# A hybrid attention and delta-rule layer: queries loaded two tiles ahead, the attention's other loads spread over its tiles, three differences of the last stage back in their place

## The chip, the cores and the metric

One core of one Trainium2 chip. The metric is the device time of one execution in microseconds (us); the kernel before takes 1301.49 us, the median of 3 runs (1301.42 to 1302.32).

## What is computed

One layer over a sequence of 1024 positions of width 1024. A normalised input goes through one projection; its columns feed two mixers, a banded attention (8 heads of 64, each chunk of 64 positions sees itself and 8 chunks before, with a learned bias by distance) and a gated delta rule (4 heads of 128, a recurrence over chunks). Their outputs are joined and projected, and a feed-forward with a squared ReLU follows:

```python
u = rms_norm(h, mix_norm_gain[layer])
proj = u @ w_in[layer]
...
mixed = jnp.concatenate([o_att, o_dn], axis=-1) @ w_out[layer]
h = h + mixed
z = rms_norm(h, ffn_norm_gain[layer]) @ w_ff1[layer]
h = h + jnp.square(jax.nn.relu(z)) @ w_ff2[layer]
```

In the attention, per head: scores of normalised q and k, plus the bias, masked to the band, softmax, times v.

## The kernel before, in words

The kernel runs in stages on the one core: the projections (to about 361 us), attention and delta rule together (to about 575), the output projection (to about 671), the first matrix of the feed-forward (ff1, to about 977) and the second (ff2, to about 1290), then the last outputs. Large products are made of three matmuls each: an operand is split into a high part (a cast on ScalarE, line 204, the names that end in _h) and a low part (the difference on VectorE, line 205, names in _l), and high x high, high x low and low x high are summed.

**What orders the work.** TensorE's (PE's) instructions run in the order in which the kernel writes them. VectorE (DVE), ScalarE (ACT), GpSimd (POOL) and SyncE (SP, which issues nearly all DMAs) are ordered by a scheduler behind the kernel, which works from where an instruction is written, from its inputs and from the tile buffers that it needs. Each engine then works through its own list in order: an instruction that waits holds up all that stand behind it on that engine. With `tc.issue_after(x)` the kernel makes an instruction wait in that order for x.

**Attention (`attention`).** The heads are worked in two groups g = 0, 1, the positions in eight tiles t of 128; a tile (g, t) is named t00 to t17. For a tile, `start` (line 885) loads the queries t.._q: two DMAs of 256 KB from q_dr, into a buffer of which there are two (only t11 has another place). For each half pp of a tile, `score` makes the scores on PE (line 916, t.._sb and t.._sa, with the keys ks), VectorE and ScalarE make the softmax, PE transposes it (lines 976 and 992, t.._tpb, t.._tpa), multiplies by the values vt (line 1015, t.._o), and turns the output (line 1037, t.._on). Between these stand the steps of the delta rule: merges of triangular blocks (m.., l.., among them m1_tp at lines 674 and 676 and l_p at line 641), and the chunk steps (c0 to c7, among them c_pv at line 517, which reads c_jv).

The order of all of this on PE comes from a planner, written out in a loop over a modelled clock: at each turn it lists what could be done (score, flip, multiply, delta steps and others), with a modelled time at which each can begin, and takes the one that can begin first, or the one of highest rank of those that can. For a score that time is when its PSUM banks are free; for the very first one it is at least START, 5000 ns. `start` is called when the first half of the tile is scored, so a tile's query load is written right ahead of its first scores. At tile t02 the planner also calls `load_rest`, which writes all at once: the older biases of group 0 (biaso00 to 03), values vt2 and vt3, keys ks010 to ks013, values vt4 to vt7, keys ks100 to ks103 and ks110 to ks113. Each of the ks and vt loads is 256 KB. At t06 follow the biases of group 1.

**ff2 (`ff2`).** The 4096 inner positions are worked in four blocks kb = 0 to 3. In each the 2 x 2 block product is made of seven products instead of eight, from sums and differences of the blocks: p1, p5, p2, p3, p6, p7, p4, in this order, each of 48 matmuls (line 1430) over two halves i = 0, 1. Operands are called after product, block, side and half: p50b0_l is the low part of side b of product p5, block 0, half 0. `prep5` makes s1 = a21 + a22 and b11 = b12 - b11, `prep3` makes s1 = s1 - a11 (line 1514) and a12 = a12 - s1, `prep7` makes a21 = a11 - a21 (line 1524) and b12 = b22 - b12, all on VectorE in place, each 128 x 1024. `early` is the last split of p5: the differences of lines 1514 and 1524 are held back until that split has been issued. While block 0 begins, the last steps of ff1 still run on VectorE and ScalarE (yy7, and its store f_dr<-yy), and the loads of block 0 come in.

Of the kernel before, what the change touches and what calls it, by code (L numbers as in the profile page):

```python
# [40 lines left out]
DELTA = 71e3  # L41
LATENCY, MARGIN = 250, 400
LEAD = 0.1
START = 5000
NV = 6


# [52 lines left out]
def hymba_kernel(  # L100
# [729 lines left out]
    def attention(after, delta, values, outputs):  # L830
# [16 lines left out]
        def load_old(g):  # L847
            for i in range(4):
                b = bias_page("u", f"biaso{g}{i}")
                nc.sync.dma_start(out=b[:, 0:384], in_=bias_win[4 * g + i, :, 0:384])  # L850
                nc.gpsimd.memset(b[64:128, 0:64], NEG)
                old[g].append(b)
# [13 lines left out]
                nc.sync.dma_start(out=tl, in_=v_dr[t])  # L866
                vt.append(tl)

        def load_rest():
            load_old(0)  # L870
            load_values((2, 3))
            load_keys(0, 1)
            load_values(range(4, NT))
            load_keys(1, 0)
            load_keys(1, 1)

        keys, old, new, vt = [[[], []], [[], []]], [[], []], [[], []], []
        load_keys(0, 0)
        load_new(0)
        load_values((0, 1))  # L880

        tiles, outs = {}, {}

        def start(g, t):
            n = f"t{g}{t}"
            T = dict(n=n, k0=max(0, t - 4))
            T["kb"] = max(0, t - 1)
            if (g, t) == (1, 1):
                T["q"] = [page("on", f"{n}_q{m}", F32R) for m in range(2)]
                for r0 in (0, 64):  # L890
                    for m in range(2):
                        nc.sync.dma_start(out=T["q"][m].bitcast(F32)[r0:r0 + 64], in_=q_dr[t, :, m, g, :])
            else:
                q = page("x", n + "_q", F32R, w=DM)
                qf = q.bitcast(F32)
                for r0 in (0, 64):
                    nc.sync.dma_start(out=qf[r0:r0 + 64].rearrange("p (m c) -> p m c", m=2), in_=q_dr[t, :, :, g, :])
                T["q"] = [part(q, m) for m in range(2)]
            T["sums"] = small("t", n + "_sum", 8)
            T["nm"] = small("t", n + "_nm", 8)  # L900
            T["s"], T["p"], T["done"] = {}, {}, {}
            tiles[g, t] = T

        def product(g, T, i, bk, off, ka, kb):
# [157 lines left out]
        total, spent, deltas, begun, multiplied = sum(size), 0, 0, 0, 0  # L1062
        ready, later, live = [], [], {}
        banks = clock.banks
        groups = delta
        fed = next(groups)

# [15 lines left out]
        while True:  # L1083
            if not any(k in live for k in "MSOF") and fed is not None:
                fed = next(groups, None)
                for k, gen in (fed or {}).items():
                    live_add(k, gen)
                continue
            todo = []
            lag = deltas < DELTA * (spent / total + LEAD)  # L1090
            for r, k in enumerate("SMOF"):
                if k in live:
                    todo.append((at(live[k][1]), (0 if lag else 6) + 0.1 * r, k))
            if multiplied < len(ready):
                t = max(ready[multiplied:multiplied + 2])
                if multiplied + 2 <= len(ready):
                    todo.append((max(t, banks["o"][0]), 1, "multiply"))
            for p in later[:1]:
                todo.append((max(p[0], banks["t"][0]), 2, "later"))
            if flipping is None and flipped < begun and flipped - multiplied < 2:  # L1100
                flipping = flip(*units[flipped])
                flipping = flipping, next(flipping)
            if flipping is not None:
                todo.append((at(flipping[1]), 3, "flip"))
            if begun < len(units) and begun - multiplied < 5 and (begun - flipped < 3):
                a = banks["a"]
                todo.append((max(a[0], a[1] - 500, a[2] - 900, START if not begun else 0), 4, "score"))
            if values_left:
                todo.append((banks["a"][0], 7, "values"))
            elif flipped == len(units) and not live.keys() - {"F"} and not any(p[1] is finish and p[2][1] < NT - 1 for p in later):  # L1110
                if outputs_gen is None:
                    outputs_gen = outputs()
                if fill < 30 and (multiplied < len(units) or later or live):
                    todo.append((banks["a"][0], 8, "outputs"))
            if not todo or (len(todo) == 1 and todo[0][2] == "outputs"):
                break
            best = min(todo, key=lambda p: (max(p[0] - clock.now, 0), p[1]))
            if best[0] > clock.now:
                clock.now = best[0]
            k = best[2]  # L1120
            if k in live:
                gen = live[k][0]
                before = clock.now
                want = next(gen, None)
                deltas += clock.now - before
                if want is None:
                    del live[k]
                else:
                    live[k] = gen, want
            elif k == "multiply":  # L1130
                for n in units[multiplied:multiplied + 2]:
                    multiply(*n)
                    pe(218 * size[multiplied])
                pe(300)
                spent += 2 * size[multiplied]
                t = give("o", on("s", 366, clock.now + LATENCY, ahead=True))
                later.append((t, finish, units[multiplied][0:2]))
                multiplied += 2
            elif k == "later":
                _, step, args = later.pop(0)  # L1140
                step(*args)
                if step is finish:
                    t = give("t", on("v", 420, pe(220), ahead=True))
                    if args[0]:
                        t = on("v", 853, on("g", 3200, on("s", 780, t)))
                        later.append((t + MARGIN, turn, args[1:]))
                        later.sort(key=lambda p: p[0])
                else:
                    give("t", on("v", 682, pe(440), ahead=True))
            elif k == "flip":  # L1150
                want = next(flipping[0], None)
                flipping = want and (flipping[0], want)
                if want is None:
                    flipped += 1
            elif k == "score":
                g, t, pp = units[begun]
                if pp == 0:
                    start(g, t)
                    if (g, t) == (0, 2):
                        load_rest()  # L1160
                    if (g, t) == (0, 6):
                        load_new(1)
                        load_old(1)
                score(g, t, pp)
                begun += 1
            elif k == "values":
                if next(values, None) is None:
                    values_left = False
                else:
                    give("a", on("s", 690, pe(5500)))  # L1170
            else:
                next(outputs_gen)
                pe(690)
                fill += 1
# [231 lines left out]
    def ff2(psw, pools):  # L1406
# [7 lines left out]

        y = {i: [wide(t, 0), wide(t, 1)] for i, t in y.items()}
        y[7] = [page2("y7", f"y7_{i}") for i in range(2)]
        side, splits = [0], []
# [4 lines left out]
        def product(name, prep, by_rows=False):  # L1422
# [11 lines left out]
            for i in range(2):  # L1434
                ab = []
                for o, src in zip("ab", prep(i)):
                    hi = page2("h" + t, f"{name}{o}{i}_h", F32R)
                    lo = page2("l" + t, f"{name}{o}{i}_l", F32R)
                    splits.append(split(src, hi, lo, nc.scalar, nc.vector)[1])
                    ab.append((hi, lo))  # L1440
                ops.append(ab)
                if not by_rows:
                    for k in range(2):
                        for q in range(4):
                            step(i, k, q)
# [13 lines left out]
        for kb in range(nb):  # L1459
# [50 lines left out]
                return s1[i], b11[i]  # L1510

            def prep3(i):
                with tc.issue_after(early):
                    tt(s1[i], s1[i], a11[i], ALU.subtract)
                tt(a12[i], a12[i], s1[i], ALU.subtract)
                return a12[i], b22[i]

# [2 lines left out]
                return s1[i], b11[i]  # L1520

            def prep7(i):
                with tc.issue_after(early):
                    tt(a21[i], a11[i], a21[i], ALU.subtract)
                tt(b12[i], b22[i], b12[i], ALU.subtract)
                return a21[i], b12[i]

# [3 lines left out]

            accumulate(1, product(f"p1{kb}", lambda i: (a11[i], b11[i])))
            accumulate(5, product(f"p5{kb}", prep5))
            early = splits[-1]
            accumulate(2, product(f"p2{kb}", lambda i: (a12[i], b21[i])))
            if last:
                merge(nc.gpsimd, 2, 1)
# [124 lines left out]
```

## Time and profile before

| | |
|---|---|
| median of 3 runs | 1301.49 us |
| the profiled execution | 1301.99 us |
| its span, first to last instruction | 1300.1 us |
| granted TensorE clock, mean | 0.984 |
| PE busy | 1252.7 us (96%) |
| VectorE busy | 931.8 us (72%) |
| ScalarE busy | 546.5 us (42%) |
| GpSimd busy | 289.9 us (22%) |
| mean DMA rate | 122 GB/s |

All times are us from the start of the span. A row of the waits names the engine and line that waited, what it waited for, the total, the number of times and the longest. A row of the timeline gives start, duration, engine, line, operation, output<-input by the program's names, and the count where like instructions are put together; the brackets hold the idle time of the engine ahead of it and what ended it. In the trace's rows buffer numbers are left out, so t_q is any tile's query page and ks any key page; matmuls overlap, so that a matmul of 0.39 us may start 0.23 us behind the one ahead. A row of the windows gives the stretch, its length, the busy time of each engine with the number of instructions, PE's granted clock (1.00 is full, 0.50 half), the busy share of the DMA engines and their rate.

### The profile page before, as it was taken

How to read it: one execution, taken by the hardware profiler on the slowest of the kernel's cores; microseconds unless marked ns; L12 is line 12 of the kernel's file. 1: busy time of each engine (PE TensorE's matmuls, PEld its weight loads, DVE VectorE, ACT ScalarE, POOL GpSimd, SP SyncE). 2: the span in 40 equal slices, each digit the busy share in tenths (PEclk: the TensorE clock that was granted, in tenths of full speed). 3: DMA queues.
4: the chain of work that ended last, by engine and by line, in shares of the span. 5: the costliest groups of instructions: out<-in, count | busy, mean ns of one | idle time of the engine just before them, and what ended most of it. 6: DMA issues, size and time to landing. Idle time of an engine off the chain costs nothing.

```text
span 1300.1 us, 18013 instructions
## 1 busy us (share of the span) xinstructions
PE 1252.7 (96%) x6686; PEld 1043.8 (80%) x6686; DVE 931.8 (72%) x1389; ACT 546.5 (42%) x898; POOL 289.9 (22%) x487
## 2 busy tenths in 40 slices
PE   9999999999979999879999999999999899999998
PEld 7778878788868988757878788888888688888886
DVE  7899978655036577662529876776668888897998
ACT  7233232232246556463436445444445343333331
POOL 4425451454013344543220000000000000000034
PEclk9999999999979999899999999999999899999999
DMA  6214354566564542123351433332259423413002
GB/s 221 68 47 143 95 150 128 100 169 171 166 210 103 160 105 76 32 85 130 109 169 46 151 118 125 101 114 93 97 194 352 166 97 126 134 61 125 9 33 97
DMA packets 135399, 158.53 MB, mean 122 GB/s; under 512 B 31760, under 2 KB 79376, under 8 KB 134800
## 3 DMA queue, kind: packets, MB, share of 16 engines
q1 hardware_dynamic: 117216, 135.11, 33.9%
q10 hardware_dynamic: 18096, 22.29, 5.0%
q8 instruction: 52, 0.85, 0.3%
q14 instruction: 35, 0.29, 0.1%
HBM read 109.91 MB, written 47.45 MB: 121 GB/s over the span
## 4 chain that ended last, share of the span: by engine, by line
PE 47%; DVE 8%; DMA 3%; ACT 2%; issue 2%; POOL 1%; POOLq 1%; SPq 0%; DVEq 0%; ACTq 0%
PE q L1334 19%; PE p L1430 19%; PE op L223 6%; DMA b<-f_dr 1%; DMA y<-h_dr 1%; PE t_o L1015 1%; DVE h L1276 1%; POOLq L1657 1%; DVE y L1502 0%; DMA h_dr<-h 0%; DVE q_0a_l L205 0%; DMA a<-in_w_ff_dram 0%; PE t_sa L916 0%; DVE y L1498 0%; ACT t_pb L955 0%
## 5 line engine op out<-in xcount | busy, mean ns | idle before, releaser
L1502 POOL TENSOR_TENSOR y<-y,y 128x1024 f32<-128x1024 f32 x6 | 19.3, 3240 | 596.5 <-DVE y L1498 577.7
L1498 DVE TENSOR_TENSOR y<-y,p 128x1024 f32<-128x1024 f32 x46 | 55.3, 1218 | 9.3 <-PE p L1430 8.4
L936 DVE CUSTOM_DVE_ANT_0 t_pb<-t_sb,biasn 128x256 f32<-128x256 f32 (+1 forms) x64 | 23.4, 404 | 41.8 <-PE t_sb L916 41.7
L223 PE MATMUL op<-mh,wo_h 128*128 128x512 f32 x128 | 50.8, 397 | 2.5 <-ACT mh L204 1.1
L223 PE MATMUL op<-ml,wo_h 128*128 128x512 f32 x128 | 50.8, 396 | 0.9 <-DVE ml L205 0.9
L223 PE MATMUL op<-mh,wo_l 128*128 128x512 f32 x128 | 49.3, 394 | 0.5 <-DVE wo_l L205 0.5
L955 ACT ACTIVATE t_pb<-t_pb,t_nm 128x256 f32<-128x256 f32 (+1 forms) x64 | 31.3, 489 | 37.8 <-DVE t_nm L947 34.4
L1221 POOL TENSOR_TENSOR op_q<-op_q 128x512 f32<-128x512 f32 x14 | 20.9, 1496 | 51.4 <-ACT op_q L1220 51.3
L916 PE MATMUL t_sb<-ks,t_q 128*128 128x256 f32 (+1 forms) x144 | 25.6, 310 | 7.0 <-DMA t_q<-q_dr 7.0
L992 PE MATMUL t_tpa<-ident,t_pa 128*128 128x128 f32 x120 | 21.7, 288 | 10.8 <-ACT t_tb L982 6.1
L1214 DVE TENSOR_TENSOR h<-op,op_x 128x512 f32<-128x512 f32 x16 | 11.0, 689 | 28.3 <-PE op L223 28.2
L223 PEld LDWEIGHTS op<-mh,wo_h 128*128 128x128 f32 x128 | 24.2, 189 | 8.7 <-ACT mh L204 1.6
L223 PEld LDWEIGHTS op<-mh,wo_l 128*128 128x128 f32 x128 | 24.3, 190 | 6.6 <-DVE wo_l L205 1.4
L223 PEld LDWEIGHTS op<-ml,wo_h 128*128 128x128 f32 x128 | 24.3, 190 | 6.1 <-DVE ml L205 1.2
L959 ACT ACTIVATE t_pa<-t_pa,t_nm 128x384 f32<-128x384 f32 (+2 forms) x48 | 26.3, 548 | 0.0
L223 PE MATMUL g_ps<-uh,wg_h 128*128 128x512 f32 x64 | 25.3, 396 | 1.0 <-ACT wg_h L204 1.0
L916 PEld LDWEIGHTS t_sb<-ks,t_q 128*128 128x128 f32 x144 | 20.4, 206 | 7.3 <-issue 7.1
L223 PE MATMUL g_ps<-uh,wg_l 128*128 128x512 f32 x64 | 25.2, 393 | 0.4 <-POOL wg_l L205 0.4
L223 PE MATMUL dq_ps<-uh,wdq_h 128*128 128x512 f32 x64 | 25.5, 398 | 0.0
L223 PE MATMUL aq_ps<-waq_h,uh 128*128 128x512 f32 x64 | 25.5, 401 | 0.0
L947 DVE CUSTOM_DVE_ANT_0 t_pa<-t_sa,biaso,t_nm 128x384 f32<-128x384 f32 (+2 forms) x48 | 24.9, 545 | 0.8 <-PE t_o L1015 0.6
L223 PE MATMUL dv_ps<-uh,wdv_l 128*128 128x512 f32 x64 | 25.4, 397 | 0.0
(1109 smaller groups left out, 4333.3 us busy)
## 6 DMA issues: line engine op xcount, KB each, us to landing
wa<-in_w_ff_dram SPq DMA_DIRECT2D x32, 512.0 KB
a<-in_w_ff_dram SPq DMA_DIRECT2D x32, 512.0 KB
b<-f_dr SPq DMA_DIRECT2D x32, 512.0 KB
f_dr<-yy ACTq DMA_DIRECT2D x16, 512.0 KB
t_q<-q_dr SPq DMA_DIRECT2D x30, 256.0 KB
f_dr<-zz ACTq DMA_DIRECT2D x13, 512.0 KB
ks<-k_dr SPq DMA_DIRECT2D x16, 256.0 KB
wo_r<-in_w_out_dram SPq DMA_DIRECT2D x16, 256.0 KB
```

The costliest lines, as they stand in the source:

```text
L223: nc.tensor.matmul(ps, a, b, start=(first and i == 0), stop=(last and i == n - 1))
L916: nc.tensor.matmul(o, q[m][:, i * P:(i + 1) * P], k[:, c], start=(m == 0), stop=(m == 1))
L936: nc.vector.tensor_tensor_reduce(sb[:, c], bk[:, c], new[g][pp][:, c], -1.0, 3.0e38, ALU.add, ALU.min, nm[:, 4 + i:5 + i])
L947: nc.vector.tensor_tensor_reduce(sa[e][:, 0:wa], bk[:, 0:wa], old[g][i][:, 384 - wa:384], -1.0, nm[:, 4 + i:5 + i], ALU.add, ALU.min, nm[: ...
L955: nc.scalar.activation(sb[:, c], sb[:, c], AF.Exp, bias=m, scale=-1.0, accum_out=T["sums"][:, 4 + i:5 + i])
L959: nc.scalar.activation(sa[e][:, 0:wa], sa[e][:, 0:wa], AF.Exp, bias=m, scale=-1.0, accum_out=T["sums"][:, i:i + 1])
L992: nc.tensor.transpose(tp[:, js], sa[e][:, js], ident)
L1221: nc.gpsimd.tensor_tensor(acc, acc, sq, ALU.add)
L1334: nc.tensor.matmul(part(ps, q), l[:, s], r, start=(k + m == 0), stop=(k == 3 and m == 2))
L1430: nc.tensor.matmul(part(ps[q], 0) if by_rows else part(ps[q // 2], q % 2), l[:, s], part(r, k), start=(i + k + m == 0), stop=(i + k + m == 4))
L1498: nc.vector.tensor_tensor(y[i][m], y[i][m], ps[m], op)
L1502: eng.tensor_tensor(y[i][m], y[i][m], y[z][m], ALU.add)
```

## The change

Three things are changed. `start` is called for the first two tiles ahead of the planner's loop, and from then on for the tile after the next, as soon as a tile's second half is scored; START goes, and a tile's scores are taken by the planner at the earliest 6000 ns of modelled time after its `start`. `load_rest` takes the number of a tile and writes a part of its loads at t = 2, 3, 4 and 6; the biases of group 1, so far loaded at t06, are its last part. In ff2 `early` goes, and the three differences (one line of `prep3`, one of `prep7`, each for two halves; of the four instructions the one on s11 keeps its place behind p5's splits) are issued where the scheduler finds their inputs ready.

```diff
-START = 5000
...
-        def load_rest():
-            load_old(0)
-            load_values((2, 3))
-            load_keys(0, 1)
-            load_values(range(4, NT))
-            load_keys(1, 0)
-            load_keys(1, 1)
+        def load_rest(t):
+
+            if t == 2:
+                load_old(0)
+                load_values((2, 3))
+            if t == 3:
+                load_keys(0, 1)
+                load_values((4, 5))
+            if t == 4:
+                load_values((6, 7))
+                load_keys(1, 0)
+            if t == 6:
+                load_keys(1, 1)
+                load_new(1)
+                load_old(1)
...
+            T["at"] = clock.now + 6000
...
+        start(0, 0)
+        start(0, 1)
...
-                todo.append((max(a[0], a[1] - 500, a[2] - 900, START if not begun else 0), 4, "score"))
+                todo.append((max(a[0], a[1] - 500, a[2] - 900, tiles[units[begun][0:2]]["at"]), 4, "score"))
...
                 g, t, pp = units[begun]
-                if pp == 0:
-                    start(g, t)
-                    if (g, t) == (0, 2):
-                        load_rest()
-                    if (g, t) == (0, 6):
-                        load_new(1)
-                        load_old(1)
                 score(g, t, pp)
                 begun += 1
+                if pp and begun + 2 < len(units):
+                    start(*units[begun + 2][0:2])
+                if pp and not g:
+                    load_rest(t + 1)
...
-                    splits.append(split(src, hi, lo, nc.scalar, nc.vector)[1])
+                    split(src, hi, lo, nc.scalar, nc.vector)
...
-                with tc.issue_after(early):
-                    tt(s1[i], s1[i], a11[i], ALU.subtract)
+                tt(s1[i], s1[i], a11[i], ALU.subtract)
...
-                with tc.issue_after(early):
-                    tt(a21[i], a11[i], a21[i], ALU.subtract)
+                tt(a21[i], a11[i], a21[i], ALU.subtract)
...
-            early = splits[-1]
```

**SyncE, the loads ahead of t02's queries.** Rows of the list: number, line, DMA, destination<-source, shape. Before:

```order
196 L859 DMA ks100_3778<-k_dr_307 128x512
197 L866 DMA vt5_3769<-v_dr_308 128x512
198 L859 DMA ks101_3780<-k_dr_307 128x512
199 L866 DMA vt6_3772<-v_dr_308 128x512
200 L859 DMA ks102_3782<-k_dr_307 128x512
201 L859 DMA ks103_3784<-k_dr_307 128x512
202 L469 DMA v_dr_308<-av7_s_3671 128x512
203 L897 DMA t02_q_3731<-q_dr_306 64x2x512 x2
204 L897 DMA t03_q_3895<-q_dr_306 64x2x512 x2
205 L866 DMA vt7_3775<-v_dr_308 128x512
```

The same place now, with what follows:

```order
196 L865 DMA vt5_3880<-v_dr_308 128x512
197 L865 DMA vt6_3987<-v_dr_308 128x512
198 L858 DMA ks102_3997<-k_dr_307 128x512
199 L858 DMA ks103_3999<-k_dr_307 128x512
200 L468 DMA v_dr_308<-av7_s_3676 128x512
201 L905 DMA t02_q_3706<-q_dr_306 64x2x512 x2
202 L905 DMA t03_q_3731<-q_dr_306 64x2x512 x2
...
211 L630 DMA l1_w0_4236<-y_dr_314 32x4x32 x3
212 L905 DMA t05_q_3982<-q_dr_306 64x2x512 x2
213 L858 DMA ks100_3993<-k_dr_307 128x512
214 L858 DMA ks101_3995<-k_dr_307 128x512
215 L630 DMA l1_w0_4236<-y_dr_314 32x4x32 x5
```

Two key loads, ks100 and ks101, have moved from ahead of t02_q to behind t05_q; the other loads ahead of t02_q are the same. t05_q, so far behind all 16 loads of l1_w0 and l1_w1, stands behind the first three. Further on, c3_jv has moved from behind the 16 l1_xa loads to ahead of them, and t06_q from ahead of them to behind.

**PE, at the first scores of t02.** t00_tpb1 transposes the softmax of t00, t00_o and t00_on are its output, m1_tp is a merge of the delta rule. Before:

```order
1466 L976 MATMUL t00_tpb1_3726<-ident_138,t00_pb1_3692 128x128 x2
1467 L916 MATMUL t02_sb0_3794<-ks000_3565,t02_q_3731 128x256 x2
1468 L916 MATMUL t02_sb0_3794<-ks001_3567,t02_q_3731 128x256 x2
1469 L916 MATMUL t02_sa0_3802<-ks000_3565,t02_q_3731 128x128 x2
1470 L916 MATMUL t02_sa1_3807<-ks001_3567,t02_q_3731 128x128 x2
1471 L1015 MATMUL t00_o_3816<-t00_tb0_3689,vt0_3581 64x128 x2
1472 L1015 MATMUL t00_o_3816<-t00_tb1_3729,vt0_3581 64x128 x2
1473 L674 MATMUL m1_tp_3821<-ident_138,l0_w0_2433 64x64 x4
1474 L676 MATMUL m1_tp_3821<-l0_w0_2433,m1_sa_3681 64x64 x4
1475 L976 MATMUL t01_tpb0_3831<-ident_138,t01_pb0_3707 128x128 x4
1476 L1037 MATMUL t00_on_3842<-ident_138,t00_pb1_3692 128x128 x2
```

Now:

```order
1466 L985 MATMUL t00_tpb1_3758<-ident_138,t00_pb1_3697 128x128 x2
1467 L1024 MATMUL t00_o_3763<-t00_tb0_3694,vt0_3581 64x128 x2
1468 L1024 MATMUL t00_o_3763<-t00_tb1_3761,vt0_3581 64x128 x2
1469 L673 MATMUL m1_tp_3768<-ident_138,l0_w0_2433 64x64 x4
1470 L675 MATMUL m1_tp_3768<-l0_w0_2433,m1_sa_3686 64x64 x4
1471 L985 MATMUL t01_tpb0_3778<-ident_138,t01_pb0_3712 128x128 x4
1472 L1046 MATMUL t00_on_3789<-ident_138,t00_pb1_3697 128x128 x2
1473 L925 MATMUL t02_sb0_3793<-ks000_3565,t02_q_3706 128x256 x2
1474 L925 MATMUL t02_sb0_3793<-ks001_3567,t02_q_3706 128x256 x2
1475 L925 MATMUL t02_sa0_3801<-ks000_3565,t02_q_3706 128x128 x2
1476 L925 MATMUL t02_sa1_3806<-ks001_3567,t02_q_3706 128x128 x2
```

t00's output, the merge, t01's transposes and t00's turning have moved ahead of t02's first scores. The scores of t03 to t05 and l1_p move behind other steps in the same manner (l1_p behind c2_pv and c2_pq); from t06 on PE's order is the same until ff2.

**VectorE, block 0 of ff2.** The rows from the first split of p5. Before:

```order
1043 L205 TENSOR_TENSOR p50a0_l_9577<-s10_0_9573,p50a0_h_9576 128x1024
1044 L1509 TENSOR_TENSOR b110_0_9469<-b120_0_9481,b110_0_9469 128x1024
1045 L1509 TENSOR_TENSOR b111_0_9471<-b121_0_9483,b111_0_9471 128x1024
1046 L1342 TENSOR_TENSOR yy7_9181<-yy7_9181,r2_7382 128x1024
1047 L205 TENSOR_TENSOR p50b0_l_9581<-b110_0_9469,p50b0_h_9580 128x1024
...
1065 L1529 TENSOR_TENSOR b211_0_9491<-b111_0_9471,b211_0_9491 128x1024
1066 L205 TENSOR_TENSOR p60a0_l_9789<-s10_0_9573,p60a0_h_9788 128x1024
1067 L205 TENSOR_TENSOR p60b0_l_9793<-b110_0_9469,p60b0_h_9792 128x1024
1068 L205 TENSOR_TENSOR p30a0_l_9718<-a120_0_9485,p30a0_h_9717 128x1024
1069 L205 TENSOR_TENSOR p30b0_l_9722<-b220_0_9493,p30b0_h_9721 128x1024
```

Now:

```order
1042 L1530 TENSOR_TENSOR a210_0_9473<-a110_0_9465,a210_0_9473 128x1024
1043 L204 TENSOR_TENSOR p50a0_l_9577<-s10_0_9573,p50a0_h_9576 128x1024
1044 L1517 TENSOR_TENSOR b110_0_9469<-b120_0_9481,b110_0_9469 128x1024
1045 L1530 TENSOR_TENSOR a211_0_9475<-a111_0_9467,a211_0_9475 128x1024
1046 L1517 TENSOR_TENSOR b111_0_9471<-b121_0_9483,b111_0_9471 128x1024
1047 L1350 TENSOR_TENSOR yy7_9181<-yy7_9181,r2_7382 128x1024
1048 L1521 TENSOR_TENSOR s10_0_9573<-s10_0_9573,a110_0_9465 128x1024
1049 L204 TENSOR_TENSOR p50b0_l_9581<-b110_0_9469,p50b0_h_9580 128x1024
...
1064 L204 TENSOR_TENSOR p30a0_l_9718<-a120_0_9485,p30a0_h_9717 128x1024
1065 L204 TENSOR_TENSOR p30b0_l_9722<-b220_0_9493,p30b0_h_9721 128x1024
1066 L1535 TENSOR_TENSOR b211_0_9491<-b111_0_9471,b211_0_9491 128x1024
1067 L204 TENSOR_TENSOR p60a0_l_9789<-s10_0_9573,p60a0_h_9788 128x1024
```

a210, a211 and s10 (its difference with a11) have moved ahead of p50b0_l; p30a0_l and p30b0_l have moved ahead of b211 and of the splits of p6. On ScalarE p20a0_h has moved ahead of p50b1_h, and both ahead of the store f_dr<-yy. On PE all of p3 now stands ahead of p6 (before, part of p6 stood between the halves of p3), and the first high x high pair of p2 ahead of the last 22 matmuls of p5. In blocks 1 to 3 the differences on a21 stand among the splits of the p4 ahead, and s10 behind the first half of p5's splits.

More of the change, by code (lines that the diff above doesn't have):

```diff
@@ L880, in attention @@
         load_values((0, 1))
+        load_rest(1)
         tiles, outs = {}, {}
@@ L1416, in ff2 @@
         y[7] = [page2("y7", f"y7_{i}") for i in range(2)]
-        side, splits = [0], []
+        side = [0]
         def load_h(t, j, hf, m):
```

## The prediction

> **What bounds the kernel now.** I read the page first, then TensorE's waits, then single stretches of the timeline. The page:
>
> ```profile
> span 1300.1 us, 18013 instructions
> PE 1252.7 (96%) x6686; PEld 1043.8 (80%) x6686; DVE 931.8 (72%) x1389; ACT 546.5 (42%) x898; POOL 289.9 (22%) x487
> ```
>
> TensorE (PE) is busy for 96% of the span, so a time is won only where PE stands still or runs at half clock. Its waits, longest total first (line, releaser, total us, times, longest):
>
> ```profile
> PE t_sb L916 <- DMA t_q<-q_dr: 7.0, 1, 7.0
> PE t_tpa L992 <- ACT t_tb L982: 6.1, 5, 3.1
> PE p L1430 <- DVE p30b_l L205: 4.7, 1, 4.7
> ```
>
> The first row is one wait: the scores of attention tile t02 wait for its queries. The third is one wait too: product p3 of block 0 of ff2 waits for the low half p30b0_l. The change touches these two places. The windows (us from the start, length, PE busy with instructions, granted clock, DMA share, GB/s) show what follows each wait:
>
> ```profile
> 364.71:371.69 6.98, 0.01 (x1) 0.68 1.06 332
> 371.69:384.32 12.63, 12.63 (x74) 0.50 0.50 139
> 551.56:554.98 3.42, 1.74 (x16) 1.00 0.00 0
> 554.98:558.40 3.42, 1.95 (x18) 1.00 0.00 0
> 575.47:578.88 3.41, 1.60 (x6) 1.00 0.52 165
> 578.88:582.29 3.41, 3.21 (x11) 0.50 0.26 79
> 1015.72:1020.42 4.70, 0.00 (x1) 0.87 0.24 71
> 1020.42:1026.03 5.61, 5.61 (x13) 0.50 0.92 310
> 1030.00:1260.00 230.00, 230.00 (x1016) 1.00 0.27 88
> ```
>
> After each of the two waits PE runs at clock 0.50: for 12.63 us in the attention, for 5.61 us in ff2. The two windows from 551.56 and the two from 575.47 bound what it takes. With 1.68 us idle of 3.42 (3.42 less 1.74) the clock stayed 1.00; with 1.81 idle of 3.41 the next 3.41 us ran at 0.50. I use 1.75 us idle in one such window as the point at which it falls. The last row says that blocks 1 to 3 of ff2 have no idle PE at all.
>
> **The queries.** PE around the wait:
>
> ```profile
> 364.00 0.71 PE L976 MATMUL t_tpb<-ident,t_pb 128*128 128x128 f32 x2
> 371.69 1.19 PE L916 MATMUL t_sb<-ks,t_q 128*128 128x256 f32 x4 [6.97 <-DMA t_q<-q_dr]
> 373.56 1.12 PE L1015 MATMUL t_o<-t_tb,vt 128*64 128x128 f32 x8
> 374.61 0.63 PE L674 MATMUL m_tp<-ident,l_w 64*64 64x64 f32 x4
> 375.17 1.11 PE L676 MATMUL m_tp<-l_w,m_sa 64*64 64x64 f32 x8
> 376.21 1.11 PE L976 MATMUL t_tpb<-ident,t_pb 128*128 128x128 f32 x4
> 377.40 1.20 PE L916 MATMUL t_sb<-ks,t_q 128*128 128x256 f32 x4
> ```
>
> And SyncE's queue ahead of the load (start, duration):
>
> ```profile
> 359.79 0.32 SPq L859 DMA_DIRECT2D ks<-k_dr  x1
> 361.08 0.41 SPq L859 DMA_DIRECT2D ks<-k_dr  x1
> 364.53 2.51 SPq L897 DMA_DIRECT2D t_q<-q_dr  x4
> ```
>
> Two things change. First, of the loads that load_rest spreads, only two, ks100 and ks101 (the rows at 359.79 and 361.08), leave their place ahead of t02_q; vt4 to vt6, ks102 and ks103 stay. t02_q does not come two tiles earlier: its buffer is one of two and is free only when t00's last scores are done. What it gains is two places. The four t_q issues take 2.51 us, 0.63 each, so two places are 1.3 us; by bytes, 2 x 256 KB at the 332 GB/s of the window's first row are 1.6. I take 1.3, since the issues and not the bytes pace the queue: t02_q lands at about 371.69 - 1.3 = 370.4.
>
> Second, PE's own order changes: t00_o, m1_tp, t01_tpb0 and t00_on now stand ahead of t02's first scores. These are the rows from 373.56 up to 377.40, 3.84 us at half clock, 1.92 at full. Their inputs are computed from scores and transposes that PE had done by 364.71, so they come within the wait: 364.71 to 370.4 is 5.7 us, of which 1.9 is now work. If the clock falls as before, the work behind 377.40 starts 1.3 + 3.84 = 5.1 us earlier. I take that. The lower end is 1.3 (the moved work isn't ready before the queries land); the upper is a clock that doesn't fall: then the rest of the 12.63 us, 12.63 - 3.84 = 8.8 at half clock, takes 4.4, PE is through at 374.8 instead of 384.32, and 9.5 us are won.
>
> Does the clock fall? Ahead of t00_o the last transposes have to be copied out of PSUM, for which I allow 1 us (an estimate); with the 1.9 of work the wait left over is about 367.7 to 370.4, 2.7 us in one piece. Counted back from the end of the half clock at 384.32 in steps of 3.413, windows end at 367.25 and 370.67, so it lies within one window, over the 1.75. I take the fall, at 3 in 4.
>
> What could take the gain back stands on SyncE later. The rows that bear on it:
>
> ```profile
> 379.38 1.17 SPq L897 DMA_DIRECT2D t_q<-q_dr  x2
> 387.31 0.33 SPq L701 DMA_DIRECT2D c_jv<-dv_dr  x1
> 415.30 0.55 SPq L635 DMA_DIRECT2D l_xa<-a_dr  x1
> 403.30 1.05 PE L517 MATMUL c_pv<-c_jv,m_yb 128*128 128x128 f32 x8
> 416.32 1.17 PE L641 MATMUL l_p<-l_w,l_xa 32*32 32x32 f32 x32
> ```
>
> t05_q now stands behind three of the l1_w loads and waits for t03's last scores, with ks100 and ks101 behind it; c3_jv stands ahead of the 16 l1_xa loads and waits for c1_pv; t06_q stands behind them. Queued behind are l1_w and l1_xa, and PE's l_p (row at 416.32) waits for these. By the rows: c3_jv can go when c1_pv ends, 403.30 + 1.05 - 5.1 = 399.3; 17 issues of 0.64 then last to 410.2; l_p comes at 416.32 - 5.1 = 411.2, and later still, since c2_pv and c2_pq now stand ahead of it. So about 1 us to spare and nothing lost. Released by PE's own earlier work (c2_jv at 387.31 waits for c0_pv), this chain moves forward with PE.
>
> **The differences of ff2.** VectorE, ScalarE and PE in block 0:
>
> ```profile
> 986.14 1.22 DVE L205 TENSOR_TENSOR p50a_l<-s,p50a_h 128x1024 fp32r<-128x1024 f32 x1
> 987.27 2.35 DVE L1509 TENSOR_TENSOR b<-b,b 128x1024 f32<-128x1024 f32 x2
> 990.68 1.22 DVE L205 TENSOR_TENSOR p50b_l<-b,p50b_h 128x1024 fp32r<-128x1024 f32 x1
> 1001.38 1.23 DVE L205 TENSOR_TENSOR p20a_l<-a,p20a_h 128x1024 fp32r<-128x1024 f32 x1 [2.67 <-ACT p20a_h L204]
> 1019.15 1.22 DVE L205 TENSOR_TENSOR p30b_l<-b,p30b_h 128x1024 fp32r<-128x1024 f32 x1
> ```
>
> ```profile
> 998.92 0.37 ACTq L1343 DMA_DIRECT2D f_dr<-yy  x1
> 1000.30 1.05 ACT L204 CAST p20a_h<-a 128x1024 fp32r<-128x1024 f32 x1
> ```
>
> ```profile
> 993.41 0.39 PE L1430 MATMUL p<-p50b_l,p50a_h 128*128 128x512 f32 x1
> 993.64 0.39 PE L1430 MATMUL p<-p50b_h,p50a_l 128*128 128x512 f32 x1
> 1020.42 0.80 PE L1430 MATMUL p<-p30b_l,p30a_h 128*128 128x512 f32 x1 [4.70 <-DVE p30b_l L205]
> 1044.49 0.39 PE L1430 MATMUL p<-p70b_h,p70a_h 128*128 128x512 f32 x1
> ```
>
> VectorE starts one such instruction every 1.13 us (986.14 to 987.27), and has no gap from 986 to 998. Three differences (a210, a211, s10) now run ahead of p50b0_l: it ends at 991.90 + 3 x 1.13 = 995.3, and PE, which wants it at 993.41, waits 1.9 us. That wait is new. Queued behind p50b0_l on VectorE are the low halves of p50a1 and p50b1; half a product is 24 matmuls of 0.227 (993.41 to 993.64), 5.4 us, so these come in time.
>
> What is won lies behind it. VectorE now fills the 2.67 us in which it waited, and p30a0_l and p30b0_l stand ahead of b211 and of both p60 splits. ScalarE now has p20a0_h ahead of the store f_dr<-yy (998.92, which waits for a load) and p20b0_h right behind it: 999.3 + 1.05 lets p20b0_l start at about 1000.5, and the difference s11 behind it at 1001.6. From there ten instructions of 1.13 precede p30a0_l's start, so p30b0_l ends near 1001.6 + 11 x 1.13 + 1.22 = 1015.3. PE wants it after p5 and p2, four half products: 995.3 + 21.8 = 1017.1. It is there 1.8 us early. So the 4.70 us and the half clock behind it (5.61 us at 0.50, 2.8 lost) go. Four products of 48 matmuls, 43.5 us, from 995.3 put the start of p7 at 1038.8 in place of 1044.49: 5.7 us won if the clock stays full. If the new 1.9 us fall into one window (they must hold 1.75; by the place of the window about even), one window at half clock costs 3.41 / 2 = 1.7, as at 578.88. I take it as falling: 4.0 won. Ends: 5.7, and minus 3.6 (the new wait and its window, with the 4.70 still there because ScalarE's casts hold p30b0_l up). Blocks 1 to 3 have the same moves, at most four instructions ahead of a split, 4.5 us. PE has no idle time there in 230 us, so its operands lie ready ahead of it; I cost the moves at nothing under that cover. If it were under 4.5 us deep, what is missing would be a new wait in each of three blocks.
>
> **Sum.** -5.1 - 4.0 = -9.1. The profiled execution took 1301.99 us (1.9 around its span), 0.5 above the median of 1301.49; I subtract from the median: 1292.4.
>
> **A rule against the clock falling.** The Trainium skill, "TensorE: Matmul & The Clock Gate" (its section on why this matters for your kernels), asks for no idle gaps over about 3 us between bursts, as one idle window is what brings half clock back. By that rule neither the 2.7 nor the 1.9 would do it, and the time would be that of rival (a). The trace disagrees: at 575.47 the window's 1.81 us were enough.
>
> **Rivals.** (a) The clock stays full in both places, since the gaps fall across two windows or need to be longer: -9.5 - 5.7 = -15.2, 1286.3. Against it the windows above; for it that both gaps are near the point. Chance 0.15. (b) The change doesn't do what it says: most loads of load_rest still stand ahead of t02_q, and the work moved ahead of its scores isn't ready, so PE still waits until 370.4 and only 1.3 is won there: -1.3 - 4.0, 1296.2. For it the three queued rows of SyncE; against it that PE had these inputs during the wait. 0.20. (c) Slower: c3_jv or t05_q waits on SyncE, and the l1_xa loads behind come late for l_p. SyncE does stand like that: between t_q at 379.38 and c2_jv at 387.31 it waited nearly 7 us. Each us that c3_jv issues after about 400.3 is a us of PE, and from 1.75 on up to two windows of half clock more (3.4). The 9.1 are lost if it issues after about 406; at 411, say, 10.7 + 3.4 less 9.1 is +5, 1306.5. The spare time is 1 us, but PE itself releases all it waits for. 0.07. (d) ff2 at its lower end, +3.6, with -5.1 before it: 1300.0, no change. 0.10. The forecast keeps 0.48.
>
> **Numbers.** Forecast 1292.4, its own range 1290 to 1295. For 8 in 10 the range reaches up to (b) and halfway to (d), 1298.5, and down to (a), 1286.3. A measurement of this kernel can tell about 0.2%, 2.6 us: faster means under 1298.9. Forecast, (a) and nearly all of (b) are faster, 0.78; (d) and a little of (b) the same, 0.13; (c) and the upper tail of (d) slower, 0.09.
>
> **What would show it.** The wait t_sb <- t_q shrinks from 7.0 to about 2.7 and t_o, m_tp, t_tpb run ahead of it; the half clock begins later and the stretch behind is 5 us earlier. In ff2 the wait p <- p30b_l goes, a row p <- p50b_l of about 1.9 comes, and p7 starts 4 to 6 us earlier relative to p5. I am wrong if PE's waits name l_p <- l_xa, if p30b_l stays, or if 1030 to 1260 is no longer without idle PE.

## The result, and the profile after

The changed kernel takes 1294.8 us (median of 4 runs, 1294.54 to 1296.4) beside 1301.9 of the kernel before in the same runs: ratio 0.9943, 95% interval 0.9926 to 0.9961. Its profiled execution has a span of 1292.9 us (before 1300.1) and a mean granted clock of 0.986 (before 0.984). It was run twice more beside the experiments: 1295.97 us (ratio 0.9954, 0.9940 to 0.9968) and 1295.73 us (0.9949, 0.9932 to 0.9965). So it is faster by about 0.5%, 6 to 7 us, where 9.1 were forecast.

PE's waits in the changed kernel, in the order of the earlier list (line numbers are 8 or 9 higher behind the edits, one lower ahead of them):

```profile
PE t_tpa L1001 <- ACT t_tb L991: 6.1, 5, 3.1
PE t_tpa L1001 <- DVE t_ta L1006: 3.5, 1, 3.5
PE t_sb L925 <- DMA t_q<-q_dr: 2.4, 1, 2.4
PE p L1438 <- DVE p50b_l L204: 1.8, 1, 1.8
PE t_tpb L985 <- ACT t_on L1053: 1.8, 3, 1.0
PE l_p L649 <- ACT l_w L653: 1.4, 1, 1.4
PE l_p L640 <- ACT l_s L643: 1.4, 1, 1.4
```

The wait for t02's queries is down from 7.0 to 2.4. The wait for p30b_l has gone and one for p50b_l has come. The waits at t_tpa are as before. The stretch at t02 on PE's timeline:

```profile
365.13 0.44 PE L1024 MATMUL t_o<-t_tb,vt 128*64 128x128 f32 x4
365.95 0.44 PE L1024 MATMUL t_o<-t_tb,vt 128*64 128x128 f32 x4 [0.38 <-DVE t_tb L991]
366.32 0.41 PE L673 MATMUL m_tp<-ident,l_w 64*64 64x64 f32 x4
366.66 0.68 PE L675 MATMUL m_tp<-l_w,m_sa 64*64 64x64 f32 x8
367.27 0.66 PE L985 MATMUL t_tpb<-ident,t_pb 128*128 128x128 f32 x4
367.76 0.38 PE L1046 MATMUL t_on<-ident,t_pb 128*128 128x128 f32 x2
370.52 1.23 PE L925 MATMUL t_sb<-ks,t_q 128*128 128x256 f32 x4 [2.38 <-DMA t_q<-q_dr]
```

The work that stood behind the wait runs ahead of it at full clock, 365.13 to 368.14, and PE then waits 2.38 us. SyncE issued the queries at 363.50 (before 364.53). The windows of PE in the changed kernel (the rows at 1.00 stand ahead of three of those at half clock):

```profile
365.62:369.03 3.41, 2.19 (x22) 1.00 1.06 336
369.03:372.44 3.41, 1.92 (x9) 0.50 1.13 219
370.52:379.27 8.75, 8.75 (x50) 0.50 0.74 199
413.40:416.82 3.42, 2.05 (x55) 1.00 1.03 241
416.82:423.64 6.82, 6.82 (x51) 0.50 0.77 262
427.06:430.47 3.41, 2.38 (x43) 1.00 0.02 5
430.47:433.88 3.41, 3.41 (x19) 0.50 0.31 77
553.35:556.76 3.41, 3.41 (x20) 0.50 0.01 2
700.12:703.54 3.42, 3.42 (x10) 0.50 0.50 152
```

The clock fell at the queries' wait as before, but the stretch is 8.75 us of work and not 12.63. The fall came at 369.03, in the middle of the wait (368.14 to 370.52), and the window ahead of it holds only 1.22 us idle (3.41 less 2.19). In exchange the stretches from 430.47, 553.35 and 700.12 are at half clock; the kernel before ran at full clock behind its waits at 431.30 and 553.30 and at 700. In ff2, VectorE and PE:

```profile
991.74 1.22 DVE L1521 TENSOR_TENSOR s<-s,a 128x1024 f32<-128x1024 f32 x1
992.87 1.22 DVE L204 TENSOR_TENSOR p50b_l<-b,p50b_h 128x1024 fp32r<-128x1024 f32 x1
999.02 1.23 DVE L204 TENSOR_TENSOR p20b_l<-b,p20b_h 128x1024 fp32r<-128x1024 f32 x1 [1.52 <-ACT p20b_h L203]
1012.65 1.22 DVE L204 TENSOR_TENSOR p30b_l<-b,p30b_h 128x1024 fp32r<-128x1024 f32 x1
```

```profile
1037.35 0.39 PE L1438 MATMUL p<-p70b_h,p70a_h 128*128 128x512 f32 x1
```

p50b0_l ends at 994.09 and holds PE up for 1.78 us; p30b0_l ends at 1013.87 and holds up nobody; p7 starts at 1037.35. Where the 7.14 us between the two spans lie, stage by stage (each stage from the start of its first matmul to that of the next; idle is its length less PE's busy time in the windows view):

| stage | before | changed | difference | idle before, changed |
|---|---|---|---|---|
| to the end of t00_tpb1 | 364.71 | 365.20 | +0.5 | |
| attention from there | 209.53 | 206.20 | -3.3 | 26.6, 22.8 |
| output projection and ff1, to p5 | 418.72 | 420.35 | +1.6 | |
| ff2, p5 to p7 | 51.53 | 45.60 | -5.9 | 4.8, 1.8 |
| the rest | 255.60 | 255.60 | 0.0 | |

In the attention the whole gain is idle time: PE is busy there for 182.9 us before and 183.4 in the changed kernel, so what the shorter stretch behind the queries saved at half clock was given back at half clock elsewhere.

### The profile page after: what moved, and what is told of

It reads as the page before. It is cut to its first block, busy times and chain, and to the rows that moved or that the text cites. A ratio compares the mean times of both kernels' runs of the same rounds, so it can differ in the third digit from the quotient of the medians.

```text
span 1292.9 us, 18011 instructions
## 1 busy us (share of the span) xinstructions
PE 1252.5 (97%) x6686; PEld 1043.8 (81%) x6686; DVE 929.4 (72%) x1388; ACT 546.3 (42%) x899; POOL 288.8 (22%) x487
## 4 chain that ended last, share of the span: by engine, by line
PE 51%; DVE 6%; ACT 2%; DMA 2%; issue 1%; POOL 1%; POOLq 1%; SPq 0%; DVEq 0%; ACTq 0%
PE q L1342 22%; PE p L1438 20%; PE op L222 6%; PE t_o L1024 1%; DMA wa<-in_w_ff_dram 1%; POOLq L1662 1%; DMA wo_r<-in_w_out_dram 0%; DVE y L1510 0%; PE t_sa L925 0%; DMA h_dr<-h 0%; DVE y L1506 0%; ACT t_pb L964 0%; ACT t_pa L968 0%; PE t_sb L925 0%; DVE p43b_l L204 0%
## 5 line engine op out<-in xcount | busy, mean ns | idle before, releaser
L222 PE MATMUL dq_ps<-ul,wdq_h 128*128 128x512 f32 x64 | 25.3, 395 | 0.0
```

What stands on the lines that cost most here:

```text
L222: nc.tensor.matmul(ps, a, b, start=(first and i == 0), stop=(last and i == n - 1))
```

## The experiments

### The two halves apart: e1 and e2

e1 is the kernel before with only the change's edits in ff2 (`early` and `splits` taken out). e2 is the changed kernel with those put back, so that it holds the attention's part alone.

```diff
 e1, on the kernel before:
-                with tc.issue_after(early):
-                    tt(s1[i], s1[i], a11[i], ALU.subtract)
+                tt(s1[i], s1[i], a11[i], ALU.subtract)
...
-                with tc.issue_after(early):
-                    tt(a21[i], a11[i], a21[i], ALU.subtract)
+                tt(a21[i], a11[i], a21[i], ALU.subtract)
```

> The kernel before with the three differences of ff2 put back, the attention as before. Theory (order on VectorE): the wait p <- p30b_l of 4.7 us and the half clock behind it go, a wait p <- p50b_l of about 1.8 us comes, and p7 starts 4 to 6 us earlier after p5: 1296 to 1298 us beside about 1301.5 of the kernel before. Rival (the differences only move the wait about, the gain of the whole change lies in the attention): within 2 us of the kernel before.

> The changed kernel with the three differences held back behind p5's splits again, so the attention's part alone. Theory: t_sb <- t_q waits about 2.4 us, p <- p30b_l keeps its 4.7; 2 to 5 us faster than the kernel before, depending on which later gaps fall into one window of the clock (each at half clock costs about 1.7). Rival (the gain lies in ff2): within 1 us.

e1: 1297.32 us beside 1302.24, ratio 0.9960 (0.9947 to 0.9973), so 3.5 to 6.9 us faster. e2: 1300.19, ratio 0.9978 (0.9966 to 0.9990), 1.3 to 4.4 us faster. Both theories hold, and both rivals fall: each half gives something. By the medians ff2 gives the larger part (4.9 against about 2 us), though the two intervals overlap. The product of the two ratios, 0.9938, is close to the three of the whole (0.9943, 0.9954, 0.9949). In e1's trace p7 starts 47.20 us behind p5, against 45.60 in the changed kernel, with the same list on VectorE and the same wait. The two kernels, PE's windows around that wait, e1 first:

```profile
992.39:995.80 3.41, 1.63 (x8) 1.00 1.05 398
995.80:999.21 3.41, 3.41 (x9) 0.50 1.04 407
```

```profile
990.25:993.67 3.42, 2.12 (x10) 1.00 1.05 401
993.67:997.08 3.41, 2.93 (x13) 1.00 1.05 402
```

In e1 the 1.78 us lay within one window, and the next ran at half clock; in the changed kernel a window's end cut them into 1.30 and 0.48, and none did. The difference, 1.6, is the price of one window (3.41 / 2 = 1.7). Four more traces have this wait of 1.8 us (a1, a2, e6, e10); in each a window's end cut it, the largest piece was 1.4, and the clock stayed full.

### The attention's part, in two: e3 and e4

e3 is e2 with all of load_rest written at t = 2 again: PE's order is the changed one, ks100 and ks101 stand ahead of t02_q as before. e4 is the kernel before with the loads spread: its queries start as before, PE keeps its old order at t02, and ks100 and ks101 stand behind.

```diff
 e3, on e2:
             if t == 2:
                 load_old(0)
                 load_values((2, 3))
-            if t == 3:
                 load_keys(0, 1)
-                load_values((4, 5))
-            if t == 4:
-                load_values((6, 7))
+                load_values(range(4, NT))
                 load_keys(1, 0)
+                load_keys(1, 1)
             if t == 6:
-                load_keys(1, 1)
                 load_new(1)
                 load_old(1)
```

```diff
 e4, on the kernel before, with load_rest(t) as in the change:
                 if pp == 0:
                     start(g, t)
-                    if (g, t) == (0, 2):
-                        load_rest()
-                    if (g, t) == (0, 6):
-                        load_new(1)
-                        load_old(1)
                 score(g, t, pp)
                 begun += 1
+                if pp and not g:
+                    load_rest(t + 1)
```

> As the attention's part alone, but all of the loads of load_rest are written at t = 2 as before, so ks100 and ks101 again stand ahead of t02_q; PE's order is the changed one. Theory (PE's order is worth the larger part: the work that now stands ahead of the wait, the loads 1.3 us): t_sb <- t_q waits about 3.7 us instead of 2.4, and the time is about 1.3 us above that of the attention's part alone. Rival (spreading the loads is what matters): the wait stays near 7 less what is moved into it, and nothing is gained over the kernel before.

> The kernel before with the loads spread as in the change, and the queries started as before: PE keeps its old order at t02, and only ks100 and ks101 move behind t02_q. Theory: t_sb <- t_q waits about 5.7 us instead of 7.0, half clock behind it as before, 1 to 1.5 us faster than the kernel before. Rival (spreading the loads is what matters): 3 us faster or more.

The wait at t02, in e3 and in e4:

```profile
PE t_sb L921 <- DMA t_q<-q_dr: 3.9, 1, 3.9
```

```profile
PE t_sb L924 <- DMA t_q<-q_dr: 5.2, 1, 5.2
```

The waits are near those of the theory (3.7 and 5.7 expected). By time e3 is at 1300.44 (ratio 0.9986, 0.9972 to 0.9999) and e4 at 1303.25 (1.0003, 0.9990 to 1.0017): PE's order alone gains up to 3.6 us, spreading the loads alone nothing that can be told: its rival (3 us or more) is outside the interval, and the theory's 1 to 1.5 us lies at the interval's edge. Between e2 and e3, 0.25 us by their medians and about 1 by their ratios, the 1.3 us of the two loads can't be separated from noise.

### The same kernel again: a1 and a2

> The changed kernel itself, run again beside the next three. Theory (the clock is judged in windows of 3.41 us whose place differs from run to run, and each gap of 1 to 3 us costs 1.7 us or nothing by how it lies in them): idle time and work on PE by stage as in the first trace within 0.5 us, but other stretches at half clock, and a span that differs by one or two steps of 1.7 us. Rival (the half-clock stretches belong to the kernel): the same stretches after the same waits.

> The changed kernel once more, to stand beside the next three in the same hour. Theory (the clock's windows lie elsewhere in each run): idle time of PE by stage within 0.6 us of its first two traces, the stretches at half clock again not all at the same waits.

The three traces of the changed kernel have 22.8, 23.5 and 24.0 us idle in the attention; nearly all of that spread is the wait for t02's queries, 2.4, 2.8 and 3.4 us. By span they are 1292.9, 1293.7 and 1295.0 us. That idle time would agree within 0.5 or 0.6 us was missed (1.2 between the first and the third). So was the theory on the clock: all three have half clock behind the same waits, 700 us included, as the rival of a1 had it. Across kernels with the same attention the stretches do move. Behind the queries e2 had 6.8 us of half clock and not 10.2; 553 has it in the three and in e8, not in e2 and e7. e1 had 13.7 us at the queries where the kernel before, with the same attention, had 17.1.

### Which difference counts: e7 and e8

e7 holds s1 - a11 back behind the first half of p5's splits, and leaves those on a21 free; e8 the other way round.

```diff
 e7, on the changed kernel (e8: the same two lines around the difference in prep7 instead):
-                tt(s1[i], s1[i], a11[i], ALU.subtract)
+                with tc.issue_after(early):
+                    tt(s1[i], s1[i], a11[i], ALU.subtract)
...
+            early = splits[-3]
```

> The changed kernel, but the difference s1 - a11 is held back behind the first half of p5's splits; those on a21 stay free. Theory (the wait p <- p50b_l is the number of differences ahead of that split, 1.13 us each): one fewer ahead, the wait falls from 1.8 to about 0.65 us, p <- p30b_l stays away: about 1 us faster than the changed kernel, up to 2.8 where the clock fell. Rival (what is held back comes late for p3): a wait at p30b_l of 1 us or more.

> The changed kernel, but the differences on a21 are held back behind the first half of p5's splits; s1 - a11 stays free. Theory (p3 comes early because p20a0_h and p30's splits were moved ahead with the a21 differences gone from behind p5): no wait at p50b_l, since one more instruction ends at 993.0 in the kernel before's time, but p <- p30b_l of 3 to 5 us is back with its half clock, and the time is 3 to 6 us above the changed kernel. Rival (s1's early difference is what brings p3 early): no wait at p30b_l, 1 to 2 us faster than the changed kernel.

In e7 PE waits at p50b_l for:

```profile
PE p L1438 <- DVE p50b_l L204: 0.7, 1, 0.7
```

One difference fewer ahead, 1.1 us less: as the theory had it. The time, 1294.71 us (ratio 0.9941, 0.9926 to 0.9956) beside 1295.97 of the changed kernel in the same runs, agrees with 1 us but doesn't show it. e8 takes 1299.44 us (0.9982, 0.9968 to 0.9996), 3.7 above the changed kernel beside it: the time that the theory gave, but not at the place. p30b_l isn't waited for; the wait is this one, and ScalarE's timeline shows why:

```profile
PE p L1438 <- ACT p20b_h L203: 4.0, 1, 4.0
```

```profile
988.89 1.05 ACT L203 CAST p50b_h<-b 128x1024 fp32r<-128x1024 f32 x1
997.10 0.37 ACTq L1351 DMA_DIRECT2D f_dr<-yy  x1
997.56 1.01 ACT L1504 COPY y<-p 128x1024 f32<-128x1024 f32 x1 [7.61 <-DMA y<-h_dr]
998.47 1.05 ACT L203 CAST p20a_h<-a 128x1024 fp32r<-128x1024 f32 x1
1000.32 1.05 ACT L203 CAST p20b_h<-b 128x1024 fp32r<-128x1024 f32 x1
```

ScalarE stands still for 7.6 us at the store f_dr<-yy, which waits for a load of y, and p20a0_h and p20b0_h are behind it. In the changed kernel p20a0_h, a copy of y, p50b1_h and another copy (990.42 to 994.22) run ahead of the store, so that behind it p20b0_h comes first, at 997.94:

```profile
990.42 1.04 ACT L203 CAST p20a_h<-a 128x1024 fp32r<-128x1024 f32 x1
997.53 0.37 ACTq L1351 DMA_DIRECT2D f_dr<-yy  x1
997.94 1.05 ACT L203 CAST p20b_h<-b 128x1024 fp32r<-128x1024 f32 x1 [3.72 <-DVE p50b_l L204]
```

So the gain of ff2 hangs on what ScalarE does ahead of that store. The a21 differences matter through the scheduler's order: held back, they leave p20a0_h behind the store; free, they let it stand ahead. Why the scheduler orders so was not looked into.

### The rest of the queries' wait: e6, e9, e10, e11

e6 holds each part of load_rest back until the queries of its tile have been issued; e9 is e6 with e7's edit. e10 gives the queries a third buffer and takes two scratch pages of the delta rule (`pp`) to make room; e11 is e10 with e7's edit.

```diff
 e6, on the changed kernel (T["load"] is the query DMA of a tile; the line that keeps it is left out):
...
-                    load_rest(t + 1)
+                    if 1 < t + 1 < NT - 1:
+                        with tc.issue_after(tiles[0, t + 1]["load"]):
+                            load_rest(t + 1)
```

```diff
 e10, on the changed kernel:
-    slots = {"x": 2, ... "pp": 7, ...
+    slots = {"x": 3, ... "pp": 5, ...
```

> The changed kernel, but the loads of load_rest for tile t are held back until the queries of t have been issued, so that the values, keys and biases really stand behind t02_q. Theory (t02_q is late because of what is queued ahead of it): t_sb <- t_q waits less than 0.5 us and the half clock behind it goes; 2 to 6 us faster than the changed kernel. Rival (t02_q is late because its buffer comes free late, or the loads now held back are missed in their turn): the wait stays over 1.5 us, or waits for biaso, vt or ks of the same size come.

> The changed kernel with both: the loads behind the queries and s1 - a11 behind the first half of p5's splits. Theory: the two gains add, 3 to 8 us faster than the changed kernel, 10 to 15 us faster than the kernel before. Rival (they are taken back by later waits or by the clock): no more than 1 us faster than the better of the two alone.

> The changed kernel with three query buffers in place of two (and two scratch pages of the delta rule fewer, to make room): t02's queries are loaded right behind t01's, without waiting for t00's last scores. Theory (the wait left over is the time that the load takes from the moment its buffer is free): no wait t_sb <- t_q of over 0.5 us, none of the half clock that began at 369 to 372; idle time in the attention 2 to 3 us less, 2 to 5 us faster than the changed kernel. Rival (the work behind is bound by later waits, or the scratch pages are missed): the idle time comes back at l_p or t_tpa, no more than 1 us faster.

> Three query buffers, and s1 - a11 held back behind the first half of p5's splits. Theory: both gains add, 3 to 7 us faster than the changed kernel, 10 to 14 us faster than the kernel before. Rival (given back to the clock or to later waits): no more than 1 us faster than three buffers alone.

e6: 1294.41 us (ratio 0.9944, 0.9929 to 0.9960), 1.6 below the changed kernel beside it by medians, and e9 1295.13 (0.9950, 0.9937 to 0.9962): no gain to be told, and the wait is still 1.8 us, as the rival had it. The windows of all engines ahead of the landing and up to it (the last two columns are the DMA share and GB/s), e6 first, then the changed kernel:

```profile
360.00:363.40 3.40, 3.40 (x25) 2.71 (x24) 0.41 (x1) 0.95 (x2) 0.63 (x2) 1.00 0.00 0
363.40:369.80 6.40, 4.16 (x36) 2.86 (x36) 3.34 (x17) 3.69 (x14) 0.47 (x2) 1.00 0.86 202
```

```profile
360.00:363.50 3.50, 3.50 (x26) 2.76 (x25) 0.39 (x1) 0.95 (x2) 0.82 (x4) 1.00 1.01 379
363.50:370.50 7.00, 4.18 (x36) 2.85 (x35) 3.35 (x17) 3.68 (x14) 0.49 (x2) 0.90 1.07 337
```

In e6 the DMA engines did nothing at all for the 3.4 us before the queries were issued, and from there to t02's first scores it still took 6.4 us, against 7.0 behind a full queue. So what is queued ahead on the DMA engines costs 0.6 us. The rest is the load itself, and when it can start: when t00's last scores leave the buffer free, as e10 shows. Whether t03's queries, issued 1.4 us behind t02's, slow that load was not tried.

e10 takes that wait away. With a free buffer t02's queries are issued at 303.83, 60 us earlier. The kernel takes 1291.10 us (ratio 0.9919, 0.9899 to 0.9939), 4.6 below the changed kernel beside it, and e11 1288.96 (0.9913, 0.9890 to 0.9936), the fastest. PE at t02 in e10:

```profile
368.33 0.38 PE L1046 MATMUL t_on<-ident,t_pb 128*128 128x128 f32 x2
368.47 0.72 PE L925 MATMUL t_sb<-ks,t_q 128*128 128x256 f32 x4
369.02 0.56 PE L925 MATMUL t_sa<-ks,t_q 128*128 128x128 f32 x4
```

No wait, and 0.72 us for what took 1.23 at half clock. Its attention takes 200.24 us, with 21.6 idle, against 206.20 to 207.37 with 22.8 to 24.0. Idle time falls by only 1.2 to 2.4 us, since l_p waits longer (1.7 and 0.7 in place of 1.4); the other 4.7 or so is half clock: none behind the queries (8.75 us at 0.50 before, so 4.4), and the rest later. That e11 adds to e10 what e7 saves (1.1) fits the medians, 2.1 apart, and isn't shown by the intervals.

## Why the prediction was right, point by point

- **The queries' place in SyncE's list.** Right in size: issued 1.0 us earlier, landing forecast at 370.4, seen at 370.52.
- **PE's order.** Right: t00_o, m1_tp, t01_tpb0 and t00_on ran within the wait, which was 2.4 us (2.7 forecast). By the waits this and not the loads is the larger part: 7.0 falls to 3.9 in e3 and to 5.2 in e4. By time their intervals overlap.
- **The clock behind it.** It fell, as taken at 3 in 4, and lasted over the work forecast: 8.75 us against 8.8. The reason given did not hold. The windows were taken to end where they ended in the trace before; here one ended at 369.03 and cut the wait in two, 0.9 and 1.5 us. By the point of 1.75 us idle in one window the clock would have stayed full, and it fell behind 1.22. So this step came out by luck. By the end of that stretch PE was 5.05 us ahead (379.27 against 384.32; 380.04 against 385.18 at the transposes behind it, where both kernels have done the same work), as the step "5.1 us earlier. I take that" had it.
- **"So about 1 us to spare and nothing lost."** This step failed: of the 5.1 only 3.3 were left at the end of the attention in the first trace. The loads for l_p were in time, and none of PE's waits names them. What took the gain back were waits that my list didn't hold, behind PE's new order: l_p behind ScalarE's l_s waits 1.4 in place of 0.7 (0.7 in e1 and e4 with the old order, 1.4 in e2 and e3 with the new), and two more gaps brought half clock, at 430.47 and 553.35, at 1.7 us each, against one window saved elsewhere. I had costed the half clock where the change acts and taken all other gaps as they were.
- **ff2's new wait.** Right: 1.78 us at p50b_l (1.9 forecast), p50b0_l at 994.09 where 995.3 less the 1.2 us by which p5 starts earlier is 994.1. e7 confirms the price of one difference.
- **ff2's gain.** Right in mechanism; p30b0_l ended at 1013.87, 1014.1 forecast on the same footing. The term of 4.0 was mis-sized by the clock: the new wait was cut by a window's end, the clock stayed full, and 5.9 us were won (5.7 was the other end). e1 has the case that I took, at 4.3.
- **Blocks 1 to 3 of ff2.** Right: costed at nothing, and what stands behind the start of p7 takes 255.6 us in both kernels.
- **700 us.** A half-clock window in ff1, 1.5 us, was in no term.
- **Sum.** -3.3 - 5.9 + 1.6 + 0.5 = -7.1 where I had -9.1: the attention 1.8 too good, ff2 1.9 too bad, and 2 us of half clock and a later start from stages that the change doesn't touch. That the first two cancel is luck. Rival (a) fell at the queries and held at p50b_l; (b) and (c) fell; of (d), ScalarE's casts do decide ff2 (e8), but here they came in time.

## What to carry to other kernels

When a load is late, look first at when its buffer comes free and how long it takes alone; holding back everything queued ahead of it made the load 0.6 us shorter here, a third buffer made the kernel 4.6 us faster. Work that can run in a wait is worth moving there even if the wait stays. And cost a gap of 1 to 3 us with the half clock that can follow it, wherever in the kernel the change shifts such gaps, since that is as large as the gap itself and moves between runs.

## What the runs showed of the hardware

The granted clock changes on a fixed grid: from 300 us to the end of the work, all its changes in a trace lie a multiple of 3.413 us apart (in the kernel before 367.25, 384.32, 418.45 and 425.28 are 5, 10 and 2 steps apart), and the grid lies elsewhere in each run. How a gap is cut by it decides much, but no single amount of idle time in a window fits all places. The kernel before has a fall that the point of 1.75 us doesn't allow, at l_p:

```profile
415.04:418.45 3.41, 2.62 (x49) 1.00 0.46 105
418.45:421.86 3.41, 3.41 (x39) 0.50 0.67 165
```

Here 0.79 us idle was followed by half clock, and in the changed kernel 1.37 and 1.03 (the windows from 413.40 and 427.06). In ff2 1.4 us (e10, 987.17 to 990.59) was not, and 1.78 (e1) was. At the wait of 3.1 us ahead of t_tpa, 1.89 us (e11, 547.12 to 550.53) was not, and 2.16 (a1, 550.35 to 553.77) was. What else runs in the window seems to count; that was not tried. The Trainium skill, "TensorE: Matmul & The Clock Gate" (section on why this matters for your kernels), warns of gaps over about 3 us; here the measurement decides for less.

Coming back takes longer behind some work than behind other. The 8.75 us behind the queries were all busy and all at 0.50, among them two whole windows (372.44 to 379.27); in e1 one window of 512-column matmuls was enough. Whether the transposes and small matmuls of the attention are the reason was not tried.

Matmuls with one column may count as idle. Before the half clock at 700.12 PE shows hardly a gap:

```profile
696.51 1.84 PE L1298 MATMUL hcol<-ones,acc 128*128 128x1 f32 x16
698.21 0.49 PE L1342 MATMUL q<-t2h,q_0a_h 128*128 128x512 f32 x1
698.54 0.40 PE L1342 MATMUL q<-t2l,q_0a_h 128*128 128x512 f32 x1
699.09 0.50 PE L1342 MATMUL q<-t2h,q_0a_l 128*128 128x512 f32 x1 [0.16 <-DVE q_0a_l L204]
```

The window from 696.71 to 700.12 holds 1.5 us of the 16 matmuls of one column and 0.16 idle. The same stretch was at half clock in six of the fourteen traces, always right behind these matmuls. That they are the cause is argued, not shown, and they alone don't decide it: in six others (the kernel before, e1, e4, e6, e7, e11) all 16 lie within one window too, and the next is at full clock.
